# A state recurrence moved from per-head steps to whole tiles on two engines, and a filter cut into token chunks

## The chip, the cores and the metric

The kernel runs on one core of a Trainium2 chip. The metric is the device time of one execution, in microseconds (us). The kernel before takes 2790.79 us (median of 3 runs, 2787.46 to 2793.94). The engines are named as the profile names them: PE (TensorE, matrix products), DVE (VectorE), ACT (ScalarE), POOL (GpSimd) and SP (SyncE, which here issues the DMAs). Each works through its own queue in order.

## The reference, cut to what matters

Two layers of a mixer run over 128 context tokens and 1024 latent tokens of width 1024. Each layer normalises and modulates `x` to `h`, projects it, and computes three branches, which are gated, merged and added to `x`:

```
y_conv = ba * short_conv(ca * xa, conv_w) * silu(ga)     # 3 taps along the tokens
o_na   = neighbourhood attention (latent) or plain attention (context)
s_new  = exp(b_last) * s + sum over the chunk of k~ v    # gated linear attention: state per head
o      = q~ s + (masked q k) v                           # what a chunk reads of the state
merged = g_conv*(y_conv @ wb[0]) + g_na*(y_na @ wb[1]) + g_gla*(y_gla @ wb[2])
x      = x + gate * (merged @ w_out)
```

The linear attention has 4 heads, with a state of 64 x 128 each, and runs in both directions. The changed lines compute the state recurrence and the three taps.

## The kernel before, in words

All large products are made of float32 pairs (a rounded part `hi` and its remainder `lo`), three matmuls each. A weight block is loaded to `wraw` by SP, rounded to `whi` by ACT and its remainder `wlo` is made by POOL (`split_w`, L182 and L183); each of the three tiles has three buffers. `mode_a` multiplies one weight block of 128 columns with one chunk of 384 tokens: 24 matmuls into a `ps` bank, of which there are two. The third matmul of each such product is the first that reads `wlo`. A bank is free again when its result has been read ("evacuated").

The tokens are cut into 3 chunks of 384. The convolution runs over 4 blocks of 128 features. In a block PE first makes `xa` and `ca` for each chunk (ACT copies `xa`, DVE multiplies the two to `u`, L1289), then `ba` and `ga` for each chunk (DVE makes `y`, L1301, and, behind ACT's tanh, `th`, L1309; POOL multiplies the two, L1310). Between the halves DVE filters `u` to `cv` over all 1154 columns (L1292 to L1294).

Beside this main work runs a side work in the same PE queue: the linear attention (`gla`) and then the neighbourhood attention. A planner (`Pace`) counts the expected time of PE's main work and lets the side work take a step whenever its credit reaches one; `pace.wait(us)` lets the side work pause for so much of the planner's time. When `gla` ends, the planner sets the rate of the attention's steps so that they end some 20 us before the main work does. PE's order is that of the code. The order of the other engines is set by a scheduler.

`gla` goes over 9 chunks of 128 tokens and leaves in `su` what each chunk adds to the state (L1121). Then comes the recurrence: 8 steps, forward in partitions 0 to 63 and backward in 64 to 127. In a step the new state `gs` is the old one times `dec` plus `su` (L1161, for each head and direction one DVE instruction on 64 x 128), and the old state times `al` is written to `su` (L1163 on POOL for the backward half, L1166 on ACT for the forward half). The state's tiles have four buffers in turn. Behind the pause PE multiplies `su` with the queries and DVE adds the result to `o` (L1193). `o` is then normalised, behind a branch on a flag (`fi`) that every engine takes.

Of the kernel before, what the change touches and what calls it, by code (L numbers as in the profile page):

```python
# [7 lines left out]
F32 = mybir.dt.float32  # L8
# [3 lines left out]
ALU = mybir.AluOpType  # L12
# [9 lines left out]
T = TP + TL  # L22
NT = T // 128
NCH = 3
CH = 384
# [4 lines left out]
GH = 4  # L30
DK = 64
DV = 128
# [80 lines left out]
def hybrid_step(ctx: ExitStack, tc: tile.TileContext, io: dict):  # L113
    nc = tc.nc
    act, dve, gps, pe, sp = nc.scalar, nc.vector, nc.gpsimd, nc.tensor, nc.sync
    pace = Pace()
# [27 lines left out]
    C = {}  # L144
# [3 lines left out]
    def rsqrt(v, n, scale, tag):  # L148

        a = st.tile([128, n], F32, name="rs_a", tag=f"rsa{tag}")  # L150
        dve.tensor_scalar(a, v, scale, EPS, op0=ALU.mult, op1=ALU.add)  # L151
        y = st.tile([128, n], F32, name="rs_y", tag=f"rsy{tag}")
        gps.tensor_tensor(y, a, mhalf[:, 0:n], op=ALU.pow)  # L153
        u = st.tile([128, n], F32, name="rs_u", tag=f"rsu{tag}")
        dve.tensor_tensor(u, y, y, op=ALU.mult)
        dve.tensor_tensor(u, u, a, op=ALU.mult)
        dve.tensor_scalar(u, u, -0.5, 1.5, op0=ALU.mult, op1=ALU.add)
        r = st.tile([128, n], F32, name="rs_r", tag=f"rsr{tag}")
        dve.tensor_tensor(r, y, u, op=ALU.mult)
        return r  # L160
# [25 lines left out]
    def load_w(pieces, nk, lo_engine=gps):  # L186
        return split_w(*raw_w(pieces, nk), lo_engine)
# [35 lines left out]
    def mode_a(wts, src, nk, c):  # L223

        wh, wl = wts
        ps = mm.tile([128, 512], F32, name="ps", tag="mm")
        n = 0
        for k in range(nk):
            hh, hl = src[c][0][:, k, :], src[c][1][:, k, :]
            for a, b in ((wh, hh), (wh, hl), (wl, hh)):  # L230
                mul_(ps[:, 0:CH], a[:, k, :], b, 0.163, start=n == 0, stop=n == 3 * nk - 1)
                n += 1
        return ps[:, 0:CH]
# [294 lines left out]
    def layer(l):  # L528
# [21 lines left out]
        def side():  # L550
            yield from gla(l, d)
            left = main0 + main_us - pace.main
            pace.rate = NH * 23 / max(left - 20.0, 40.0)
            yield from attention(l, d)
# [15 lines left out]
        for m in range(4):  # L570
            conv(l, m, win, fw, cvp, d.yd[0])
# [458 lines left out]
    def gla(l, d):  # L1030
# [5 lines left out]
        dec = g0.tile([128, NT, GH], F32, name="dec")  # L1036
# [114 lines left out]
        S = g1.tile([128, GH, DV], F32, name="gs", tag="la")  # L1151
        sp.dma_start(S[0:64], io["state_fwd"][0, l].rearrange("h k v -> k h v"))
        sp.dma_start(S[64:128], io["state_bwd"][0, l].rearrange("h k v -> k h v"))
        for i in range(8):
            nS = g1.tile([128, GH, DV], F32, name="gs", tag=("qk1", "la")[i % 2])
            for s, c in ((0, i), (1, 7 - i)):
                r = slice(64 * s, 64 * s + 64)
                u = su[r, c, :].rearrange("p (h v) -> p h v", h=GH)
                if i < 7:
                    for h in range(GH):  # L1160
                        dve.scalar_tensor_tensor(nS[r, h], S[r, h], dec[r, c + 1, h:h + 1], u[:, h], op0=ALU.mult, op1=ALU.add)  # L1161
                if s:
                    gps.tensor_tensor(u, S[r], al[r, c + 1, :, 0:1].to_broadcast([64, GH, DV]), op=ALU.mult)  # L1163
                else:
                    for h in range(GH):
                        act.mul(u[:, h], S[r, h], al[r, c + 1, h, 0:1])  # L1166
            S = nS
# [13 lines left out]
        for c in range(NCH):  # L1181
            o3 = g2.tile([128, 3, BW], F32, name="o3", tag="o3", bufs=3)
            sp.dma_start(o3, d.oid[c * CH:(c + 1) * CH, :].rearrange("(t p) c -> p t c", p=128))
            O.append(o3)
        yield from pace.wait(20.0)
        for c in range(1, NT):
            load_q(c + 2)
            qt, o = qts[c], O[c // 3][:, c % 3, :]
# [11 lines left out]
        for c, o3 in enumerate(O):  # L1200
# [3 lines left out]
            r = rsqrt(red, 12, 1.0 / DV, "q")  # L1204
# [67 lines left out]
    def segs(c):  # L1272

        return ((0, 128, 0), (128, 256, 130)) if c == 0 else ((0, 384, CH * c + 2),)

    def conv(l, m, win, fw, cvp, yd):
        wx = load_w([win(XA + m * 128, 128)], KD)
        wc = load_w([win(CA + m * 128, 128)], KD)
        u = cvp.tile([128, T + 4], F32, name="u", tag="u", bufs=1)
        gps.memset(u[:, 0:1], 0.0)  # L1280
        gps.memset(u[:, 129:131], 0.0)
        gps.memset(u[:, T + 3:T + 4], 0.0)
        for c in range(NCH):
            ps = mode_a(wx, H, KD, c)
            xa = cvp.tile([128, CH], F32, name="xa", tag="xa")
            act.copy(xa, ps)
            ps = mode_a(wc, H, KD, c)
            for o, n, p in segs(c):
                dve.tensor_tensor(u[:, p + 1:p + 1 + n], ps[:, o:o + n], xa[:, o:o + n], op=ALU.mult)  # L1289
        cv = cvp.tile([128, T + 2], F32, name="cv", tag="cv", bufs=1)  # L1290
        w = lambda i: C["conv_w"][:, l, m, i:i + 1]
        dve.tensor_scalar(cv, u[:, 0:T + 2], w(0), None, op0=ALU.mult)  # L1292
        dve.scalar_tensor_tensor(cv, u[:, 1:T + 3], w(1), cv, op0=ALU.mult, op1=ALU.add)
        dve.scalar_tensor_tensor(cv, u[:, 2:T + 4], w(2), cv, op0=ALU.mult, op1=ALU.add)  # L1294
        wb = load_w([win(BA + m * 128, 128)], KD)
        wg = load_w([win(GA + m * 128, 128)], KD)
        for c in range(NCH):
            ps = mode_a(wb, H, KD, c)
            y1 = fw.tile([128, CH], F32, name="y1", tag="y1")
            for o, n, p in segs(c):  # L1300
                dve.tensor_tensor(y1[:, o:o + n], ps[:, o:o + n], cv[:, p:p + n], op=ALU.mult)  # L1301
            ps = mode_a(wg, H, KD, c)
            keep(yd)(c, m, silu2_times(ps, y1, fw, "th"))

    def silu2_times(ps, y1, fw, tag):

        th = fw.tile([128, CH], F32, name="th", tag=tag)
        act.activation(th, ps, ACTF.Tanh, scale=0.5)
        dve.scalar_tensor_tensor(th, th, 1.0, ps, op0=ALU.add, op1=ALU.mult)  # L1309
        gps.tensor_tensor(th, th, y1, op=ALU.mult)  # L1310
        return th

    def keep(yd):
        def f(c, m, y):
            sp.dma_start(yd[m * 128:(m + 1) * 128, c * CH:(c + 1) * CH], y)
        return f
# [225 lines left out]
```

## Time and profile before

| | |
|---|---|
| median of the timed runs | 2790.79 us |
| the profiled execution | 2797.96 us |
| its span, first to last instruction | 2796.2 us |
| PE busy | 2710.4 us (97%) |
| DVE busy | 1192.1 us (43%) |
| POOL busy | 1038.9 us (37%) |
| ACT busy | 954.0 us (34%) |
| granted TensorE clock, mean | 0.991 |

PE is the engine that sets the time: it is busy 97% of the span. The three other engines have time over on the mean, but each works in order, and PE waits wherever one of them delivers late. So the places where PE sits idle are to be looked for, and what stood in front of the late instruction on its engine. The first layer's convolution and recurrence stand around 350 to 600 us, its attention from about 600 to 1130 us; the second layer has the same 1385 us later.

### The profile page before, as it was taken

The numbers are of one execution on the slowest core, as the hardware profiler recorded it, in microseconds if no ns is written. First come the engines' busy times: TensorE is split into PE (matmuls) and PEld (weight loads), VectorE is DVE, ScalarE is ACT, GpSimd is POOL, SyncE is SP. The second block draws the span as 40 slices with busy tenths as digits, with TensorE's granted clock in tenths as the row PEclk, the third lists the DMA queues.
The fourth block names the chain that finished last, engine by engine and source line by source line (L and its number), as shares of the span: only waits on it lengthen the run. The fifth ranks groups of instructions, "written<-read, shape, count | busy, mean of one in ns | idle before, by whom it ended". The sixth has DMA issues, their size and how long they took to land. (4 is left out here: it accounts for less than half of the span.)

```text
span 2796.2 us, 47972 instructions
## 1 busy us (share of the span) xinstructions
PE 2710.4 (97%) x18548; PEld 2654.7 (95%) x18548; DVE 1192.1 (43%) x2391; ACT 954.0 (34%) x1820; POOL 1038.9 (37%) x884
## 2 busy tenths in 40 slices
PE   6999999999999999999989999999999999999999
PEld 4999999999999999999989999989999999999999
DVE  5345335545444443335173453364553334433341
ACT  6244322223444433312152442222344343342121
POOL 0343233453574431167343332333642112212852
PEclk8999999999999999999999999999999999999999
DMA  7444672364665653555243447623655555435551
GB/s 234 119 137 121 202 230 71 114 178 139 169 180 154 171 155 92 180 177 168 89 127 111 126 121 227 212 67 126 173 151 148 142 139 155 135 109 177 168 180 69
DMA packets 455740, 415.26 MB, mean 149 GB/s; under 512 B 84740, under 2 KB 422028, under 8 KB 455248
## 3 DMA queue, kind: packets, MB, share of 16 engines
q1 hardware_dynamic: 455504, 412.13, 49.9%
q8 instruction: 146, 2.39, 0.4%
q14 instruction: 90, 0.74, 0.1%
HBM read 292.04 MB, written 136.74 MB: 153 GB/s over the span
## 5 line engine op out<-in xcount | busy, mean ns | idle before, releaser
L131 PE MATMUL ps<-hhi,whi 128*128 128x384 f32 x2496 | 851.5, 341 | 20.5 <-DVE y L1301 6.5
L131 PE MATMUL ps<-hhi,wlo 128*128 128x384 f32 x2496 | 848.1, 340 | 0.3 <-PEq L1196 0.3
L131 PE MATMUL ps<-hlo,whi 128*128 128x384 f32 x2496 | 848.1, 340 | 0.0
L183 POOL TENSOR_TENSOR wlo<-wraw,whi 128x1024 fp32r<-128x1024 f32 (+2 forms) x172 | 369.3, 2147 | 828.8 <-ACT whi L182 751.2
L131 PE MATMUL ps<-wlo,hhi 128*128 128x256 f32 (+1 forms) x1984 | 567.9, 286 | 7.0 <-DVE wlo L183 7.0
L131 PE MATMUL ps<-whi,hhi 128*128 128x256 f32 (+1 forms) x1984 | 567.9, 286 | 4.4 <-DVE ro L617 2.4
L131 PE MATMUL ps<-whi,hlo 128*128 128x256 f32 (+1 forms) x1984 | 567.5, 286 | 0.0
L131 PEld LDWEIGHTS ps<-hhi,whi 128*128 128x128 f32 x2496 | 471.2, 189 | 29.7 <-DVE th L1309 6.7
L131 PEld LDWEIGHTS ps<-hlo,whi 128*128 128x128 f32 x2496 | 471.1, 189 | 2.1 <-issue 1.4
L131 PEld LDWEIGHTS ps<-hhi,wlo 128*128 128x128 f32 x2496 | 471.2, 189 | 1.8 <-issue 0.9
L131 PEld LDWEIGHTS ps<-wlo,hhi 128*128 128x128 f32 x1984 | 380.9, 192 | 9.0 <-DVE wlo L183 8.1
L131 PEld LDWEIGHTS ps<-whi,hhi 128*128 128x128 f32 x1984 | 381.0, 192 | 7.4 <-PE ps L131 3.1
L131 PEld LDWEIGHTS ps<-whi,hlo 128*128 128x128 f32 x1984 | 380.9, 192 | 0.6 <-issue 0.3
L182 ACT CAST whi<-wraw 128x1024 fp32r<-128x1024 f32 (+1 forms) x200 | 189.5, 949 | 323.8 <-PE ps L131 251.2
L964 DVE TENSOR_TENSOR ptl<-psb,pth 128x640 fp32r<-128x640 f32 x128 | 105.3, 823 | 189.4 <-ACT pth L963 189.3
L935 ACT ACTIVATE prob<-prob,mn 128x640 f32<-128x640 f32 x128 | 106.3, 830 | 190.4 <-DVE mn L934 190.1
L934 DVE CUSTOM_DVE_ANT_0 prob<-psb,bt 128x640 f32<-128x640 f32 x128 | 105.2, 822 | 97.6 <-PE psb L131 84.2
L296 POOL TENSOR_SCALAR adapr<-wraw,scond 128x256 f32<-128x256 f32 x112 | 110.3, 984 | 94.2 <-DMA wraw<-in_w_ada 44.7
L131 PE MATMUL ps<-yh,whi 128*128 128x384 f32 x384 | 131.2, 342 | 4.4 <-DVE mx L1389 3.0
L153 POOL TENSOR_TENSOR rs_y<-rs_a,mhalf 128x12 f32<-128x12 f32 (+2 forms) x42 | 78.3, 1864 | 141.0 <-DVE rs_a L151 134.9
L131 PE MATMUL ps<-yl,whi 128*128 128x384 f32 x384 | 130.0, 339 | 0.0
L131 PE MATMUL ps<-yh,wlo 128*128 128x384 f32 x384 | 130.0, 339 | 0.0
(220 smaller groups left out, 3605.2 us busy)
## 6 DMA issues: line engine op xcount, KB each, us to landing
wraw<-in_w_in SPq DMA_DIRECT2D x88, 512.0 KB, 4.4
gd<-gt SPq DMA_DIRECT2D x144, 192.0 KB, 2.2
gl<-gd SPq DMA_DIRECT2D x144, 192.0 KB, 2.7
wraw<-in_w_gate SPq DMA_DIRECT2D x48, 512.0 KB, 4.7
wraw<-in_w_ada SPq DMA_DIRECT2D x32, 512.0 KB, 4.0
qt<-qld SPq DMA_DIRECT2D x128, 128.0 KB, 3.1
vt<-vw SPq DMA_DIRECT2D x64, 256.0 KB, 3.3
wraw<-in_w_branch SPq DMA_DIRECT2D x48, 256.0 KB, 3.0
```

Of the source, the lines that this page charges most:

```text
L131: pe.matmul(out, lhsT, rhs, **kw)
L153: gps.tensor_tensor(y, a, mhalf[:, 0:n], op=ALU.pow)
L182: act.copy(hi[:, 0:n], raw[:, 0:n])
L183: lo_engine.tensor_tensor(lo[:, 0:n], raw[:, 0:n], hi[:, 0:n].bitcast(F32), op=ALU.subtract)
L296: gps.tensor_scalar(pr, rv[:, kk], w, None, op0=ALU.mult)
L934: dve.tensor_tensor_reduce(p[:, 0:n], ps[:, lo:lo + n], bias, 1.0, 3e38, ALU.add, ALU.min, mn)
L935: act.activation(p[:, 0:n], p[:, 0:n], ACTF.Exp, bias=mn, scale=-1.0, accum_out=sums)
L964: dve.tensor_tensor(to[1], src, to[0].bitcast(F32), op=ALU.subtract)
```

## The change

Three parts, in both layers alike. First, a step of the recurrence handles all four heads with two instructions on 64 x 512, a multiply with `dec` and an add of `su`: the forward half on DVE, the backward half on POOL. Second, the pause behind the recurrence is 45 instead of 20 us of the planner's time. Third, the filter of a convolution block is made for each chunk of tokens by itself, as soon as the next chunk's `u` is there, into three tiles `cv` instead of one.

```diff
                 if i < 7:
-                    for h in range(GH):
-                        dve.scalar_tensor_tensor(nS[r, h], S[r, h], dec[r, c + 1, h:h + 1], u[:, h], op0=ALU.mult, op1=ALU.add)
+                    eng = gps if s else dve
+                    eng.tensor_tensor(nS[r], S[r], dec[r, c + 1, :].unsqueeze(2).to_broadcast([64, GH, DV]), op=ALU.mult)
+                    eng.tensor_tensor(nS[r], nS[r], u, op=ALU.add)
...
-        yield from pace.wait(20.0)
+        yield from pace.wait(45.0)
...
+        taps = {}
+
+        def filtered(c):
+
+            a = CH * c + 2 if c else 0
+            n = CH * (c + 1) + 2 - a
+            cv = cvp.tile([128, CH + 2], F32, name="cv", tag="cv", bufs=3)
+            w = lambda i: C["conv_w"][:, l, m, i:i + 1]
+            dve.tensor_scalar(cv[:, 0:n], u[:, a:a + n], w(0), None, op0=ALU.mult)
+            for i in (1, 2):
+                dve.scalar_tensor_tensor(cv[:, 0:n], u[:, a + i:a + i + n], w(i), cv[:, 0:n], op0=ALU.mult, op1=ALU.add)
+            taps[c] = cv, a
+
...
-        cv = cvp.tile([128, T + 2], F32, name="cv", tag="cv", bufs=1)
-        w = lambda i: C["conv_w"][:, l, m, i:i + 1]
-        dve.tensor_scalar(cv, u[:, 0:T + 2], w(0), None, op0=ALU.mult)
-        dve.scalar_tensor_tensor(cv, u[:, 1:T + 3], w(1), cv, op0=ALU.mult, op1=ALU.add)
-        dve.scalar_tensor_tensor(cv, u[:, 2:T + 4], w(2), cv, op0=ALU.mult, op1=ALU.add)
+            if c:
+                filtered(c - 1)
+        filtered(NCH - 1)
...
-                dve.tensor_tensor(y1[:, o:o + n], ps[:, o:o + n], cv[:, p:p + n], op=ALU.mult)
+                cv, a = taps[c]
+                dve.tensor_tensor(y1[:, o:o + n], ps[:, o:o + n], cv[:, p - a:p - a + n], op=ALU.mult)
```

Line numbers of after are up to 13 higher behind the change: `y` is L1314 there, `th` L1322 on DVE and L1323 on POOL, `u` L1303, the product of the backward state L1164. The names in the rows below are those of the tiles; a number behind one is that of its buffer.

DVE in the second convolution block of the first layer, from the last `su` (L1121) on, before:

```order
L1121 TENSOR_TENSOR su<-psm,al 128x512
L1161 SCALAR_TENSOR_TENSOR gs<-gs,dec,su 64x128 x16
L1301 TENSOR_TENSOR y_5305<-ps,cv 128x384
L1161 SCALAR_TENSOR_TENSOR gs<-gs,dec,su 64x128 x17
L1309 SCALAR_TENSOR_TENSOR th<-th,ps 128x384
L1161 SCALAR_TENSOR_TENSOR gs<-gs,dec,su 64x128 x10
L1301 TENSOR_TENSOR y_5490<-ps,cv 128x384
```

And the same place of the changed kernel:

```order
L1121 TENSOR_TENSOR su<-psm,al 128x512
L1161 TENSOR_TENSOR gs<-gs,dec 64x512
L1314 TENSOR_TENSOR y_5321<-ps,cv 128x384
L1162 TENSOR_TENSOR gs<-gs,su 64x512
L1161 TENSOR_TENSOR gs<-gs,dec 64x512
L1162 TENSOR_TENSOR gs<-gs,su 64x512
L1322 SCALAR_TENSOR_TENSOR th<-th,ps 128x384
L1161 TENSOR_TENSOR gs<-gs,dec 64x512
L1314 TENSOR_TENSOR y_5478<-ps,cv 128x384
L1162 TENSOR_TENSOR gs<-gs,su 64x512
```

In front of each evacuation (`y`, `th`) there stood 10 to 17 small steps; now there stand one to three larger instructions.

POOL at the same place, before: behind the `th` of the block's first chunk the products of the backward state, and between them the remainders `wlo` of the next block's two first weights (`wraw` and `whi` are the raw and the rounded weights):

```order
L1310 TENSOR_TENSOR th<-th,y_5219 128x384
L1163 TENSOR_TENSOR su<-gs,al 64x512 x5
L1310 TENSOR_TENSOR th<-th,y_5305 128x384
L1163 TENSOR_TENSOR su<-gs,al 64x512
L183 TENSOR_TENSOR wlo<-wraw,whi 128x1024
L1163 TENSOR_TENSOR su<-gs,al 64x512 x2
L183 TENSOR_TENSOR wlo<-wraw,whi 128x1024
L1310 TENSOR_TENSOR th<-th,y_5490 128x384
```

And in the changed kernel, behind the same first `th`:

```order
L1162 TENSOR_TENSOR gs<-gs,su 64x512
L1164 TENSOR_TENSOR su<-gs,al 64x512
L1161 TENSOR_TENSOR gs<-gs,dec 64x512
L1162 TENSOR_TENSOR gs<-gs,su 64x512
L1164 TENSOR_TENSOR su<-gs,al 64x512
L1161 TENSOR_TENSOR gs<-gs,dec 64x512
L1162 TENSOR_TENSOR gs<-gs,su 64x512
L1323 TENSOR_TENSOR th<-th,y_5321 128x384
L1164 TENSOR_TENSOR su<-gs,al 64x512
L1161 TENSOR_TENSOR gs<-gs,dec 64x512
L1162 TENSOR_TENSOR gs<-gs,su 64x512
L183 TENSOR_TENSOR wlo<-wraw,whi 128x1024
```

Six products and one `th` stood in front of the first `wlo`; now six products, four adds and one `th` do. Two more products stand between it and the second `wlo`, before and now.

PE where it first multiplies `su` with the queries (`gq2`), before in the third block's first half (row 2971 of PE's queue):

```order
L131 MATMUL ps_5592<-hlo_200,whi_5524 128x384
L131 MATMUL ps_5592<-hhi_199,wlo_5525 128x384
L131 MATMUL psm_5607<-su_3625,gq2_5434 128x128 x4
L131 MATMUL ps_5592<-hhi_199,whi_5524 128x384
L131 MATMUL ps_5592<-hlo_200,whi_5524 128x384
```

And in the changed kernel, in the third block's second half (row 3130):

```order
L131 MATMUL ps_5795<-hlo_200,whi_5706 128x384
L131 MATMUL ps_5795<-hhi_199,wlo_5707 128x384
L131 MATMUL psm_5801<-su_3625,gq2_5422 128x128 x4
L131 MATMUL ps_5795<-hhi_199,whi_5706 128x384
L131 MATMUL ps_5795<-hlo_200,whi_5706 128x384
```

The product moved back by 159 rows, and all that follows it in the side work with it; the matmuls around it are the same main work.

## Rows read from the trace of the kernel before

**Rows 1.** Busy time by stretch: recurrence and attention, first and second layer.

```profile
core 0: us, PE busy (x) PEld busy (x) DVE busy (x) ACT busy (x) POOL busy (x), PEclk, DMA share, GB/s
455.00:600.00 145.00, 137.62 (x838) 135.26 (x838) 80.56 (x124) 36.26 (x64) 68.50 (x57) 0.99 0.39 116
600.00:1130.00 530.00, 519.27 (x3255) 511.68 (x3254) 240.69 (x524) 212.33 (x415) 226.00 (x206) 0.99 0.55 153
1840.00:1985.00 145.00, 139.52 (x851) 137.16 (x850) 80.55 (x124) 37.48 (x66) 69.66 (x57) 0.99 0.38 115
1985.00:2515.00 530.00, 527.23 (x3305) 521.11 (x3304) 215.85 (x455) 213.72 (x416) 130.11 (x95) 1.00 0.52 144
```

**Rows 2.** Waits of PE, 455 to 600 us: total us, times, longest.

```profile
PE ps L131 <- DVE y L1301: 4.2, 3, 2.9
PE ps L131 <- DVE th L1309: 3.0, 1, 3.0
```

**Rows 3.** Timeline of DVE behind the last `su`: start us, us, instructions [idle before].

```profile
473.86 0.69 DVE L1121 TENSOR_TENSOR su<-psm,al 128x512 f32<-128x512 f32 x1 [1.35 <-PE psm L131]
474.58 6.95 DVE L1161 SCALAR_TENSOR_TENSOR gs<-gs,dec,su 64x128 f32<-64x128 f32 x16
481.46 0.54 DVE L1301 TENSOR_TENSOR y<-ps,cv 128x384 f32<-128x384 f32 x1
482.03 6.86 DVE L1161 SCALAR_TENSOR_TENSOR gs<-gs,dec,su 64x128 f32<-64x128 f32 x17
488.92 0.56 DVE L1309 SCALAR_TENSOR_TENSOR th<-th,ps 128x384 f32<-128x384 f32 x1
489.51 6.71 DVE L1161 SCALAR_TENSOR_TENSOR gs<-gs,dec,su 64x128 f32<-64x128 f32 x10
496.25 0.56 DVE L1301 TENSOR_TENSOR y<-ps,cv 128x384 f32<-128x384 f32 x1
```

**Rows 4.** Timeline of PE, first layer.

```profile
480.50 0.33 PE L131 MATMUL ps<-hlo,whi 128*128 128x384 f32 x1
480.67 0.33 PE L131 MATMUL ps<-hhi,wlo 128*128 128x384 f32 x1
...
482.06 0.44 PE L131 MATMUL ps<-hhi,whi 128*128 128x384 f32 x1 [0.53 <-DVE y L1301]
...
508.97 1.05 PE L131 MATMUL psm<-su,gq 128*128 128x128 f32 x8
```

**Rows 5.** Busy time and granted clock by stretch, behind the stops.

```profile
497.00:503.00 6.00, 6.00 (x26) 6.00 (x27) 0.75 (x2) 0.74 (x3) 5.38 (x4) 0.72 1.04 350
503.00:506.00 3.00, 3.00 (x19) 3.00 (x18) 0.00 (x0) 0.41 (x1) 0.00 (x0) 1.00 1.04 399
1868.00:1884.00 16.00, 11.16 (x52) 10.53 (x53) 15.24 (x31) 8.23 (x22) 6.99 (x6) 0.89 0.11 33
```

**Rows 6.** By line and shape, POOL and DVE: count | busy us, mean ns | idle.

```profile
L183 POOL TENSOR_TENSOR wlo<-wraw,whi 128x1024 fp32r<-128x1024 f32 x122 | 297.5, 2439 | 667.9 <-ACT whi L182 605.2 <-DMA bt<-t2d 19.5 <-PE ps L131 14.9
L1310 POOL TENSOR_TENSOR th<-th,y 128x384 f32<-128x384 f32 x48 | 49.3, 1027 | 80.8 <-DVE th L1309 74.0 <-issue 4.1 <-DVE rs_u L155 2.7
L1098 POOL TENSOR_TENSOR am<-am 128x512 f32<-128x512 f32 x18 | 23.0, 1280 | 101.9 <-DVE am L1097 91.8 <-PE ps L131 5.5 <-DMA qk<-qkd 4.5
L1163 POOL TENSOR_TENSOR su<-gs,al 64x512 f32<-64x512 f32 x16 | 16.9, 1061 | 21.7 <-DVE gs L1161 18.9 <-issue 2.8
L1193 DVE TENSOR_TENSOR o<-o,psm 128x512 f32<-128x512 f32 x16 | 11.0, 687 | 28.9 <-PE psm L131 26.6 <-DMA gq<-qtd 2.3
```

**Rows 7.** Timelines of DVE and POOL around a filter, first layer.

```profile
461.95 3.43 DVE L1293 SCALAR_TENSOR_TENSOR cv<-u,conv_w,cv 128x1154 f32<-128x1154 f32 x1
465.42 1.42 DVE L1294 SCALAR_TENSOR_TENSOR cv<-u,conv_w,cv 128x1154 f32<-128x1154 f32 x1
461.26 2.90 POOL L183 TENSOR_TENSOR wlo<-wraw,whi 128x1024 fp32r<-128x1024 f32 x1
```

**Rows 8.** Waits of PE in the first attention stretch, the longest.

```profile
PE psb L135 <- DVE ptl L964: 4.8, 2, 4.3
```

## The prediction

> **What bounds the kernel now.** I read the busy time by stretch first. TensorE (PE) is busy nearly always, so a change can only win what PE loses: from 455 to 600 us it is busy 137.62 of 145 us and in the same stretch of the second layer, 1840 to 1985, 139.52: 7.4 and 5.5 us idle. The two attention stretches behind them lose 10.7 and 2.8 us [rows 1]. Then the waits of PE inside the first layer's stretch, to see who ends that idle time: VectorE (DVE), with an evacuation of the convolution, `y` (L1301, 4.2 us) or `th` (L1309, 3.0 us); that is 7.2 of the 7.4 [rows 2]. The second layer runs the same code, and I take its 5.5 us for the same. PE waits nowhere for the state itself.
>
> Then DVE's timeline there, to see why an evacuation of 0.55 us comes late [rows 3]. The last `su` ends at 473.86 + 0.69 = 474.55. Behind it stand 16 small state steps (6.95 us), one `y`, 17 steps (6.86), one `th`, 10 steps (6.71), one `y`. DVE works in order, `ps` has two banks, and one product is 24 matmuls 0.17 us apart, 4.2 us [rows 4]: each evacuation may stand 4.2 us behind its product, and here about 7 us of steps stand between two of them. So PE stops at 481.53 (482.06 less its wait of 0.53), then twice more.
>
> A second loss follows: in the 6 us after the stops the granted clock is 0.72 of full (part of the time at 1.2 instead of 2.4 GHz), in the second layer 0.89 over 16 us; a stretch at full clock, like the 3 us behind the first, reads 1.00 [rows 5]. 6 x 0.28 and 16 x 0.11 give about 1.7 us each. What the change can win in the two stretches is thus 7.4 + 5.5 + 2 x 1.7 = 16 us, less the 0.2 us a layer that these waits don't explain: 15.9 us.
>
> **The state recurrence.** Behind the last `su`, DVE loses 44 steps (20.9 us, of which the three groups here are 20.5 [rows 3]) and gets 8 instructions on 64x512: four multiplies, four adds. The trace of before has neither. The nearest row is `o` (L1193, 128x512) with 0.69 us; the other end is four of the old steps at 0.43 each, 1.74 [rows 3, 6]. I take 0.69, the same element count per partition: 5.5 us where 20.9 stood. The order shows at most three of them in front of an evacuation, 2.1 us. So the old stops go, if these instructions need not wait for GpSimd (POOL).
>
> POOL gets the other half, 14 instructions a layer. The broadcast product there costs 1.06 (L1163), a sum of two full tiles 1.28 (L1098) [rows 6]. POOL's chain can't begin before 474.55, since its first add reads the last `su`. Queued behind it is what matters: `wlo` of the next block's first weights, the twelfth row of the piece of order. In front of it are four adds, six products and one `th`: 4 x 1.28 + 6 x 1.06 + 1.03 = 12.5 us; `wlo` takes 2.44 [rows 6]. It is ready at 474.55 + 14.9 = 489.5. PE without stops needs it with the third matmul of that product: 481.53 + 48 x 0.174 + 0.35 = 490.2. So with undisturbed engines it just fits: late is nothing.
>
> But they disturb each other. A filter step of DVE that takes 1.42 us alone took 3.43 beside a `wlo` on POOL, and that `wlo` took 2.90 [rows 7]. DVE's six state instructions in front of this `wlo` therefore add up to 6 x 0.69 = 4.1 us to POOL's chain: ready at 493.6, PE 3.4 us late. The second `wlo` has two more products in front of it, 2.1 + 2.4 = 4.6 us against PE's 4.2: another 0.4. Bounds of the new stop: 0 to 3.8 us a layer. I take 1.7, since POOL also idles for `th`, when DVE can pass: 3.4 us in both layers. A fall of the clock behind so short a stop is left out here; rival 1 has it.
>
> The Trainium skill says of this (SBUF — State Buffer, Who interferes with whom) that a VectorE instruction with two SBUF inputs and a GpSimd instruction that reads SBUF exclude each other, and that the later one waits for the whole of the other. The old `y` and `th` have one input in PSUM and are untouched by this rule; all new DVE instructions have two in SBUF, so it speaks against this change. The 3.43 against 1.42 agrees; by the rule in full the new stop would be at the upper bound above, without it at the lower.
>
> **The pause.** From 20 to 45 on the planner's clock. PE's first product with `su` moves back by 159 rows (the piece of order): 159 x 0.174 = 27.7 us, from 508.97 to about 530 once 7 us of stops are gone. POOL's whole chain from 474.55: 7 adds, 14 products, 2 `th`, 2 `wlo` = 9.0 + 14.8 + 2.1 + 4.9 = 30.8, with eight DVE instructions 36.3: done by 511. PE does not wait for it, 19 us to spare; with the old pause and no stops it would have come at 502 and waited 9. Behind the pause the normalisation of `o` moves from the third convolution block into the fourth, beside the sums for the next modulation. In the order each `u` still stands in front of where PE needs it; cost nothing, hidden by two `ps` banks; a late `u` there would cost 1 to 2 us a layer, which I keep for the range.
>
> Attention ends with the main work as before, but starts 27 us later: the same 72 items in some 500 instead of 530 us, 5% denser. PE's work there is the same. Its idle time, 10.7 and 2.8 us [rows 1], is a matter of which `ptl`, cast or bias load collides (4.8 us of the first are two waits for `ptl` [rows 8]); the collisions are drawn anew. From both sides: -6 (the 4.3 us wait and its clock fall vanish) to +13.5 (all idle time doubles). I take +2.
>
> **The filter by chunks.** Nine instructions for three, the same columns: six fixed parts more. 128x384 against 128x512 (0.55 and 0.69 [rows 3, 6]) leave 0.14 us for an instruction without columns: 0.8 us of DVE a block, beside PE, with DVE busy 80.6 of 145 us [rows 1]. Behind the last `u` only four of the nine are left. What is left of the first layer's `y` waits beside the stops, 4.2 - 0.5 - 2.9 = 0.8 us, lies at this place of the fourth block [rows 2]; it is in the 15.9. SP's and POOL's queues get nothing from this part.
>
> **The sum.** -15.9 + 3.4 + 2 = -10.5 us. Against the profiled execution, 2797.96 (span 2796.2 and 1.8 around it), that is 2787.5; its own time lies 7 us above the median of the timed runs, so I apply the difference to that median: 2790.79 - 10 = 2781.
>
> **Rivals.**
> 1. POOL becomes the bound in the recurrence: `wlo` 3.8 us late in each layer, and the clock falls after it as it did after 3.0 us: 2 x (3.8 + 1.7) = 11 of 15.9 us come back, with the +2 of attention: -3, 2788. For it: the 3.43 us [rows 7], and POOL's in-order queue; against: PE's slack holds if POOL gets the port at once. 0.22.
> 2. Slower: the denser attention. One mechanism: the chain from scores to `ptl` (DVE, ACT, DVE, PE, ACT, DVE) is late for its slot, since the slots are 5% closer while the weights, casts and modulation sums beside it are not. The other terms give -12.5, so it eats the gain once the idle time of the two attention stretches doubles (13.5 us more) and is a loss that can be measured from 18 us more on; at +20 the time is 2798. Against: PE idles 2.8 of 530 us in the second layer, so there is slack. 0.12.
> 3. The attention falls well: its 4.3 us wait goes too, and no `wlo` is late: -15.9 - 5: 2770. 0.14.
> 4. The change doesn't do what it says: `su` is late in spite of the pause and PE waits; needs POOL 19 us behind my sum, then no gain: 2791. 0.02.
>
> **How the numbers follow.** Forecast 0.50, 2774 to 2786 by the bounds of its terms. A measurement here tells 0.2%, 5.6 us, from no change: faster is below 2785.2, slower above 2796.4. Faster: 0.48 of the forecast, 0.14 of rival 3, some 0.06 of rival 1: 0.68. Slower: 0.11. Same: the rest, 0.21. The range goes from rival 3 to just short of rival 2: 2771 to 2795.
>
> **What would show it.** Right: no PE wait for `y` or `th` between 474 and 500 us nor at its place in the second layer; the granted clock 1.00 there; DVE busy some 15 us less around 474 to 497; a new PE wait of 0 to 4 us for POOL's `wlo` at the start of the third block; none for `su`. Wrong: a `wlo` wait over 4 us, any wait of PE for DVE's `o`, or idle time in the attention stretches above 25 us together. If the stops go and the time doesn't fall by 5 us, the attention stretches must show where it went.

## The result, and the profile after

The changed kernel takes 2837.37 us (median of 6 runs, 2827.34 to 2841.42), the one before 2790.42 beside it (6 runs, 2787.46 to 2793.94): a ratio of 1.0155, 95% interval 1.0138 to 1.0171. By the ratio it is 43 us slower (47 by the medians), where 10 us faster were forecast.

The profiled execution has a span of 2839.3 us against 2796.2. PE is busy 2721.8 instead of 2710.4 us, at a mean granted clock of 0.984 instead of 0.991; so 31.7 of the 43.1 us are idle time of PE and 11.4 are longer matmuls. The busy time by stretch says where, in the columns of [rows 1]:

```profile
455.00:600.00 145.00, 136.65 (x811) 134.32 (x810) 77.52 (x106) 32.43 (x57) 84.32 (x63) 0.96 0.29 89
600.00:1130.00 530.00, 505.06 (x3144) 497.27 (x3143) 236.56 (x508) 205.86 (x404) 227.68 (x212) 0.98 0.57 157
1840.00:1985.00 145.00, 140.04 (x858) 137.29 (x857) 65.61 (x93) 33.65 (x66) 68.60 (x55) 0.96 0.25 80
1985.00:2515.00 530.00, 510.84 (x3185) 503.08 (x3184) 222.05 (x459) 205.42 (x398) 149.80 (x113) 0.99 0.52 144
```

The second layer stands some 21 us later in the changed kernel, so that a stop of its fourth block (at 2000 us) falls out of the third stretch into the fourth. Moved by 21 us the two read:

```profile
1861.00:2006.00 145.00, 136.54 (x809) 134.00 (x808) 77.57 (x106) 32.33 (x57) 84.23 (x63) 0.96 0.29 89
2006.00:2536.00 530.00, 514.34 (x3217) 507.25 (x3216) 211.28 (x446) 209.32 (x406) 132.33 (x101) 0.99 0.52 142
```

In the recurrence PE thus idles 8.4 and 8.5 us, where [rows 1] gave 7.4 and 5.5: nothing was won. In the attention stretches it idles 24.9 and 15.7 us, where it idled 10.7 and 2.8. The waits of PE over the whole run (total us, times, longest) name them:

```profile
PE ps L131 <- DVE th L1347: 23.8, 2, 12.0
PE psb L135 <- DVE ptl L964: 9.7, 4, 4.3
PE ps L131 <- DVE u L1303: 9.7, 4, 3.2
...
PE ps L131 <- ACT xa L1300: 6.4, 3, 2.9
...
PE ps L131 <- DVE y L1314: 0.4, 1, 0.4
PE ps L131 <- POOL wlo L183: 0.4, 1, 0.4
```

The old waits for `y` and for `th` in the convolution [rows 2] are gone, and the feared wait for `wlo` is 0.4 us. In their place stand four kinds of stop, each once a layer.

**The start of attention: 12 us for `th` (L1347).** This `th` belongs to the stage behind the convolution, which stores one every 4.2 us. The timeline of SP there, first layer (start, us, instructions):

```profile
623.29 0.39 SPq L173 DMA_DIRECT2D wraw<-in_w_in  x1
...
625.89 10.11 SPq L862 DMA_DIRECT2D bt<-t2d  x16
...
636.69 0.59 SPq L877 DMA_DIRECT2D vraw<-in_cache_v  x1
...
639.74 0.45 SPq L1328 DMA_DIRECT2D y0d<-th  x1
```

And that of ACT, with what ended each idle time:

```profile
632.20 1.04 ACT L182 CAST whi<-wraw 128x1024 fp32r<-128x1024 f32 x1 [7.60 <-DMA bt<-t2d]
638.83 0.30 ACT L879 CAST vc<-vraw 128x128 fp32r<-128x128 f32 x1 [5.58 <-DMA vraw<-in_cache_v]
643.00 0.96 ACT L1346 ACTIVATE th<-ps 128x384 f32<-128x384 f32 x2 [3.87 <-DMA y0d<-th]
```

Sixteen loads of the bias tile `bt` occupy SP for 10 us; behind them stand the load of `vraw`, on which ACT waits with a cast in its queue, and the store `y0d<-th`, on which the next `th` waits for its buffer, since there are two. PE stops from 632.3 to 644.1. In the kernel before the same loads stood elsewhere:

```profile
586.05 8.81 SPq L862 DMA_DIRECT2D bt<-t2d  x16
...
596.95 0.43 SPq L1315 DMA_DIRECT2D y0d<-th  x1
```

There they stand between the last `u` of the fourth convolution block (DVE at 585.47) and the store of its first `th`, where PE waits under 1 us. The pause moved them.

**The fourth block: 3.2 us for `u`.** The normalisation of `o`, moved there by the pause, stands in front of `u` on DVE:

```profile
588.83 2.35 DVE L157 TENSOR_SCALAR rs_u<-rs_u 128x12 f32<-128x12 f32 x1
591.22 0.65 DVE L159 TENSOR_TENSOR rs_r<-rs_y,rs_u 128x12 f32<-128x12 f32 x1
591.90 1.76 DVE L1207 TENSOR_TENSOR o<-o,rs_r 128x1536 f32<-128x1536 f32 x1
593.57 0.55 DVE L1303 TENSOR_TENSOR u<-ps,xa 128x384 f32<-128x384 f32 x1
```

Its first instruction has 12 columns and takes 2.35 us, as long as the `wlo` that runs on POOL beside it from 588.54 (2.61 us).

**In front of the recurrence: 1.6 to 1.8 us for `u`.** POOL now has a state multiply in front of the all-reduce of the flag `fa`:

```profile
450.35 1.50 POOL L1161 TENSOR_TENSOR gs<-gs,dec 64x512 f32<-64x512 f32 x1
457.45 0.38 POOL L1147 PARTITION_ALL_REDUCE fa<-fm  x1 [5.59 <-PE psm L135]
457.86 0.15 DVE L1149 TENSOR_SCALAR fi<-fa 128x1 int32<-128x1 f32 x1 [6.91 <-POOL fa L1147]
```

DVE idles 6.91 us for `fa`, and `u` stands behind. The all-reduce starts 5.6 us after POOL's last instruction, as it did before the change (5.7 us there); the multiply moves it back, and the order on DVE now has the flag ahead of `gqt`, `gkt` and `u`. The Trainium skill (GPSIMD Engine Reference, Instruction dispatch) says that a freshly loaded GpSimd routine first pays about 6 us with no instruction in the profile; the 5.6 us agree, behind two instructions that configure POOL (`MODIFY_POOL_CONFIG`, at 451.8).

**In the recurrence: 2.9 us for `xa`.** DVE's and ACT's timelines, then the clock behind the stop:

```profile
487.87 1.51 DVE L1161 TENSOR_TENSOR gs<-gs,dec 64x512 f32<-64x512 f32 x1 [0.94 <-POOL su L1164]
489.42 1.67 DVE L1162 TENSOR_TENSOR gs<-gs,su 64x512 f32<-64x512 f32 x1
...
493.85 1.52 DVE L1161 TENSOR_TENSOR gs<-gs,dec 64x512 f32<-64x512 f32 x1 [2.30 <-POOL su L1164]
...
502.03 2.76 DVE L1162 TENSOR_TENSOR gs<-gs,su 64x512 f32<-64x512 f32 x1
```

```profile
504.83 2.44 ACT L1167 ACTIVATE su<-gs,al 64x128 f32<-64x128 f32 x8 [5.12 <-DVE gs L1162]
507.18 0.46 ACT L1300 COPY xa<-ps 128x384 f32<-128x384 f32 x1
```

```profile
508.00:514.00 6.00, 6.00 (x20) 6.00 (x20) 2.81 (x3) 0.00 (x0) 5.77 (x6) 0.52 0.95 320
644.00:650.00 6.00, 5.87 (x18) 5.87 (x19) 0.55 (x2) 0.00 (x0) 0.00 (x0) 0.50 1.10 307
```

Where [rows 3] had groups of steps without a gap, DVE now waits between them. A state instruction takes 1.3 to 1.7 us beside POOL and the last one 2.76 beside a `wlo` (501.53, 2.72), against 0.68 alone (at 448.04); [rows 7] had shown the same of a filter. And DVE waits for POOL: a state tile's buffer is free only when POOL's product (L1164) has read the old state. So ACT's products come late, the last ones behind the 2.76 us, and `xa` behind them. In the 6 us after this stop and after the one for `th` the clock is 0.52 and 0.50 of full (0.72 in [rows 5]), the lower of the two levels (1.2 GHz) for nearly all of the time; at the same places of the second layer it is 0.50 and 0.74.

### The profile page after: what moved, and what is told of

Read it like the earlier page. It is cut to its first block, busy times and chain, and to the rows that moved or that the text cites. A ratio compares the mean times of both kernels' runs of the same rounds, so it can differ in the third digit from the quotient of the medians.

```text
span 2839.3 us, 47971 instructions
## 1 busy us (share of the span) xinstructions
PE 2721.8 (96%) x18548; PEld 2665.4 (94%) x18548; DVE 1193.7 (42%) x2355; ACT 953.4 (34%) x1820; POOL 1086.1 (38%) x912
## 5 line engine op out<-in xcount | busy, mean ns | idle before, releaser
L131 PE MATMUL ps<-hhi,whi 128*128 128x384 f32 x2496 | 858.3, 344 | 46.1 <-DVE th L1347 23.8
L296 POOL TENSOR_SCALAR adapr<-wraw,scond 128x256 f32<-128x256 f32 x112 | 120.1, 1072 | 95.5 <-DMA gate_d<-gate_s 36.4
```

What stands on the lines that cost most here:

```text
L131: pe.matmul(out, lhsT, rhs, **kw)
L296: gps.tensor_scalar(pr, rv[:, kk], w, None, op0=ALU.mult)
```

## The experiments

Each batch has its own runs of the kernel before (medians 2795.9 to 2800.2 us); ratios are to those, with 95% intervals.

**e1, the pause alone.**

```diff
-        yield from pace.wait(20.0)
+        yield from pace.wait(45.0)
```

> The kernel before with the pause of 45 instead of 20 alone. Theory (the pause): it moves the start of attention, with its burst of bias loads in SP's queue, onto the second half of the fourth convolution block, where PE needs a th every 4.2 us, and the normalisation of o into that block's first half. Both stops of the changed kernel must be here: a wait of PE for th of about 12 us and one for u of about 3 us in each layer, with the clock falls behind them some 2 x 17 = 34 us: 2815 to 2830 us. Rival 1 (GpSimd's half of the recurrence is what costs): no new stop, 2786 to 2795. Rival 2 (the denser attention costs, wherever it starts): 2800 to 2815, in many waits under 5 us within attention.

2845.27 us, 1.0163 (1.0143 to 1.0182): 45 us slower, above the theory's band. The `th` wait at the start of attention is the theory's, and the recurrence is the old one. The `u` wait of 3 us did not come; in the fourth block PE waits for `ott` (2.8 and 2.2 us) and for `y` instead:

```profile
PE ps L131 <- DVE th L1334: 20.4, 2, 10.9
...
PE psb L135 <- DVE ptl L964: 9.1, 3, 4.1
PE ps L131 <- DVE y L1301: 8.2, 6, 2.4
PE psm L131 <- ACT pth L963: 7.2, 4, 3.2
...
PE psm L135 <- ACT ott L1214: 5.3, 3, 2.8
```

So the pause by itself costs as much as the whole change. GpSimd's half isn't needed for it, against rival 1.

**e2, the recurrence alone; e3, the filter alone; e4, the changed kernel with the pause of 20.**

```diff
-                    for h in range(GH):
-                        dve.scalar_tensor_tensor(nS[r, h], S[r, h], dec[r, c + 1, h:h + 1], u[:, h], op0=ALU.mult, op1=ALU.add)
+                    eng = gps if s else dve
+                    eng.tensor_tensor(nS[r], S[r], dec[r, c + 1, :].unsqueeze(2).to_broadcast([64, GH, DV]), op=ALU.mult)
+                    eng.tensor_tensor(nS[r], nS[r], u, op=ALU.add)
```

> The kernel before with the new recurrence alone (pause 20, filter in one piece). Theory (the pause): the old stops for y and th go (-15.9 us), the new ones for u and xa come (2 x 1.7, 2 x 2.9 and three clock falls of 1.7: +14), and no th wait at the start of attention: 2786 to 2794; if PE now comes to its first product with su before GpSimd's chain is through, a wait for su of up to 9 us a layer on top, up to 2808. Rival 1 (GpSimd's half): 2815 to 2835. Rival 2 (denser attention): 2780 to 2794, since the rate of attention is that of the kernel before.

> The kernel before with the filter by token chunks alone. The prediction priced it at nothing: 2787 to 2794, with the y wait of 0.8 us in the fourth block gone and the stops of the recurrence where they were. No theory of the loss asks for more than 2 us here.

> The changed kernel with its pause set back from 45 to 20. Theory (the pause): the th wait of 12 us and the u wait of 3 us in the fourth block go in both layers, 2 x 17 = 34 us: 2795 to 2808, the same as the new recurrence alone but for 3 us. Rival 1 (GpSimd's half): within 8 us of the changed kernel, 2829 to 2841. Rival 2 (denser attention): 15 to 25 us under the changed kernel, with the th wait still there.

e2: 2810.14 us, 1.0036 (1.0021 to 1.0051), 10 us slower. e3: 2800.60, 1.0003 (0.9989 to 1.0017), nothing. e4: 2810.04, 1.0049 (1.0028 to 1.0069), 14 us slower by the ratio (10 by the medians), with no `th` wait at the start of attention. Both fall where the theory of the pause put them, e2 with the wait for `su`. The waits of PE in e2:

```profile
PE psm L131 <- POOL su L1164: 10.5, 2, 6.1
...
PE ps L131 <- ACT xa L1287: 5.8, 2, 2.9
...
PE ps L131 <- DVE u L1290: 3.8, 2, 2.1
```

They are the `xa` wait and the first `u` wait of the changed kernel, and a wait for `su` that the longer pause covers. So the new recurrence is no gain at either pause: what it takes from DVE it loses through POOL, to 20.1 us of these waits, where `y` and `th` together cost 12.6 in the kernel before (6.5 and 6.1).

**e6, both halves of the new recurrence on DVE.**

Against e2:

```diff
-                    eng = gps if s else dve
+                    eng = dve
```

> The kernel before with the state on 64x512 instructions for both halves on DVE, nothing on GpSimd; pause 20, filter in one piece. Theory (GpSimd's half costs through DVE, ACT and the last product): the waits of PE for u behind the all-reduce, for xa and for su, which the new recurrence alone showed, all go; each DVE instruction is back at 0.68 us; 28 of them (19 us) stand where the old steps took 23, four to six in front of an evacuation, so that y and th waits of 0 to 2 us remain: 5 to 12 us faster than before. Rival (it is the form of the instructions or the tightened chain that costs, not GpSimd): the xa and u waits stay, 5 to 12 us slower than before, like the new recurrence alone.

2796.20 us, 1.0000 (0.9985 to 1.0014). The waits for `u`, `xa` and `su` are gone, as the theory said of POOL's half. But `th` costs 8.8 us (four waits, up to 3.7), more than expected, and the gain of 5 to 12 us did not come. The `th` that stops PE stands on ACT, behind products that wait for state instructions of DVE; two of these took 3.50 us beside a `wlo` there (491.43; the `wlo` 490.93, 2.73).

**e5 and e9, the changed kernel with another start of attention.** e5 puts the bias loads behind the first items' loads and hands them out; e9 takes ACT's two waits away as well.

```diff
-        load_bias(0, 0, 3)
         for i in range(2):
             ahead(i)
-        yield from pace.wait(16.0)
+        until = pace.clock + 16.0
+        for g in range(2):
+            for r in range(8):
+                load_rows(0, 0, 3, g, r)        # one of the sixteen loads
+                if r % 3 == 2 and not pace.draining:
+                    yield
+        while pace.clock < until and not pace.draining:
+            yield
...
-            act.copy(vc[:, :, 0, :], raw)                                    # e9
+            gps.tensor_copy(vc[:, :, 0, :], raw)
...
-            th = fw.tile([128, CH], F32, name="th", tag="th")                # e9
+            th = (fw, cvp)[(3 * m + c) % 2].tile([128, CH], F32, name="th", tag=("th", "xa")[(3 * m + c) % 2])
```

> The changed kernel, its pause of 45 kept, with the sixteen bias loads at the start of attention behind the loads of the first two items and handed out three at a time, a step of the planner between, within the 16 us that the kernel waits there anyway. Theory (the burst): the two th waits of 12 us go down to under 3 us each and their clock falls with them: 20 to 30 us faster than the changed kernel, so 13 to 25 us slower than the one before. Rival (attention put later is slow in itself, by its rate or by what it meets there, whatever the order of the loads): the waits stay, or come back elsewhere in attention, and the time stays within 8 us of the changed kernel.

> e5 (the changed kernel with the bias loads handed out), and two things more that the trace of e5 shows in front of the late th: the silus stage's th takes four buffers in turn instead of two (the two more are those of xa, unused by then), so that ACT need not wait for a store to land, and vc is cast on GpSimd instead of ACT, so that ACT does not stand before a load. Theory (the stop is a matter of queues at the start of attention): the th wait of 5.5 us in each layer goes to under 1, some 11 us of waits and 4 of clock less than e5: 0 to 17 us slower than the kernel before. Rival (a later attention costs whatever is done to its start): within 4 us of e5, 26 to 34 us slower than before.

e5: 2829.16 us, 1.0107 (1.0069 to 1.0144); the `th` wait falls from 23.8 to 10.7. e9: 2830.97, 1.0113 (1.0096 to 1.0131); it falls to 2.0, and the time does not. So e5 gains 13 us on the changed kernel (1.0155), between its theory and its rival, and e9 is its rival's. The wait has moved on:

```profile
PE psb L135 <- DVE ptl L968: 20.8, 5, 6.9
...
PE ps L131 <- DVE u L1313: 10.2, 4, 3.3
...
PE ps L131 <- DVE th L1357: 2.0, 2, 1.4
```

Some 35 us later SP and ACT in e9 read:

```profile
657.10 5.45 SPq L860 DMA_DIRECT2D bt<-t2d  x11
...
667.29 0.38 SPq L173 DMA_DIRECT2D wraw<-in_w_gate  x1
```

```profile
671.62 1.04 ACT L182 CAST whi<-wraw 128x1024 fp32r<-128x1024 f32 x1 [11.27 <-DMA wraw<-in_w_gate]
672.57 0.82 ACT L939 ACTIVATE prob<-prob,mn 128x640 f32<-128x640 f32 x1
```

A weight load stands on SP behind the next head's bias loads (issued at 667.29, 4.3 us before its cast starts), its cast stands on ACT in front of the exponential, and PE waits 5.8 us for `ptl`. My theory that the stop at the start was the cost fell here: removed, most of it is given back at the next load.

**e12, the same start with the pause alone.** The pause of e1 and the start of e9, on the old recurrence.

> The kernel before with the pause of 45 and the start of attention of e9 (bias loads handed out three at a time, th with four buffers, vc on GpSimd); old recurrence, filter in one piece. Theory (SP's queue, full of each head's bias loads, is what a later attention meets): the th wait is under 1 us, PE waits 5 to 7 us for ptl in each layer some 40 us later behind the next head's loads, as in e9, and the time stays 25 to 36 us over before. Rival (the th stop was the cost, and e9 kept only what the new recurrence costs): 5 to 15 us over before.

2818.66 us, 1.0083 (1.0059 to 1.0107): 23 us over before, between the two expectations. There the start does take half of the 45 us away. `ptl` costs 15.8 us (4.8 before [rows 8]), `ott` 5.2 and `y` 8.0 (6.5).

**e13 and e14, the bias tiles of the first head only.** Pause 20 and 45, with the start of e9 and without the reloads:

```diff
-                if g == 1 and j in (0, 3) and h + 1 < NH:
-                    load_bias(h + 1, *((0, 1) if j == 0 else (1, 3)))
```

> The kernel before (pause 20) with the start of attention of e9, and the bias tiles loaded for the first head only: the reloads for the seven other heads of each layer are left out, 224 loads a layer. It is the partner of e14. Theory (SP's queue): the kernel before loses little to these loads where attention starts early, so 0 to 10 us faster than before. Rival (attention itself): the same as before within 4 us.

> e13 with the pause of 45. Theory (SP's queue): without the reloads the later attention costs little, within 12 us of e13, and the ptl wait 40 us into attention is gone. Rival (attention itself, its density or its place in the queues of DVE and ACT): 25 to 36 us over e13, as e12 is over before.

Both kernels leave out loads that the result needs; they only measure. e13: 2785.59 us, 0.9963 (0.9950 to 0.9976). e14: 2807.44, 1.0038 (1.0024 to 1.0052). The reloads cost about 10 us with either pause, and the later attention still costs 22 us without them (2807.4 less 2785.6), as it cost 23 with them. So the reloads are not its cause, against my theory. In e14 a stop some 25 us into attention reads so on SP and ACT:

```profile
644.00 0.43 SPq L173 DMA_DIRECT2D wraw<-in_w_gate  x1
```

```profile
652.52 1.04 ACT L182 CAST whi<-wraw 128x1024 fp32r<-128x1024 f32 x1 [8.65 <-DMA wraw<-in_w_gate]
...
653.88 0.69 ACT L965 CAST pth<-psb 128x640 fp32r<-128x640 f32 x1
```

The load is issued right behind those of the next head's keys and values and lands 8.5 us later, and ACT holds attention's casts behind it; PE waits 4.7 us for `ptl`, and 7.2 in the second layer. With 5.5 for `ott` in the fourth block that is 17.4 of the 20.3 us by which PE idles longer in the profiled execution of e14 than in that of e13 (94.2 and 73.9); another 11.7 us there are longer matmuls. In e13 the same load is issued at 631.80, lands 3.8 us later and is not waited for: its cast starts at 645.03. The stretches around the two loads, first e13, then e14:

```profile
628.00:636.00 8.00, 8.00 (x52) 7.93 (x51) 4.22 (x8) 4.25 (x7) 2.40 (x1) 1.00 0.54 165
640.00:650.00 10.00, 10.00 (x63) 9.97 (x62) 2.12 (x6) 1.30 (x3) 0.00 (x0) 1.00 1.10 254
```

The DMA share is 0.54 in the one and 1.10 in the other, where ACT already stands at the cast (from 643.87) when SP issues the load. So in e14 the load is issued too late and meets full DMA engines. Whether an earlier load of that weight would end it was not tried.

**e7 and e8, one state step behind each evacuation.** e6, with a step's `dec` made by a small instruction that reads the last evacuated tile, and steps 4 us apart; e8 has the start of e5 as well.

```diff
+            gate[0] = st.tile([128, GH], F32, name="gz")          # behind each y, th, u
+            dve.tensor_scalar(gate[0], x[:, 0:GH], 0.0, None, op0=ALU.mult)
...
+                        dve.tensor_tensor(dg[r], dt, gate[0][r], op=ALU.add)
+                yield from pace.wait(4.0)
```

> As e6, and each step of the state takes its dec through a small instruction that reads four columns (times zero) of the last evacuated tile, so that one step stands behind each evacuation, y, th or u, not several in front of one; the steps are handed out 4 us of the planner's time apart and the pause behind them is 4.5, which puts PE's first product with su and all of attention some 14 us later than before. Theory (DVE's order bounds the recurrence, and a late attention meets the stores): no y, th, u or xa wait over 1 us between 455 and 530 us; but the burst of bias loads falls into the second half of the fourth block, a th wait of 2 to 6 us in each layer there: between 10 us faster than before and the same. Rival (the old stops come back wherever DVE is over 90% busy): waits of 5 us a layer in the third block's first half, 0 to 8 us slower.

> As e7, with the bias loads handed out as in e5. Theory: neither the old stops nor the th wait of the burst: 10 to 16 us faster than before, all that PE lost in the recurrence. Rival (attention put 14 us later costs in itself): as e7, within 3 us.

e7: 2822.91 us, 1.0084 (1.0051 to 1.0117), and 23.6 us of `th` waits are back at the start of attention. e8: 2816.26, 1.0071 (1.0047 to 1.0096), with 10.4 of them. Both theories missed. PE's first product with `su` comes at 534.7 in e7 (509.0 before), 147 rows back and not 14 us: nearly the 159 rows of the changed kernel. And the gates did not end the stops of the recurrence: in each layer of e7 PE waits 2.0 us for `th` and 2.3 behind a gate (`gz`), where the kernel before lost 4.4 to 5.9 in its two longest. Again a later attention costs.

**e10, e11 and e15, gates without a later attention.** e10 gates the last three steps only and takes their waits out of the pause; e11 adds the start of e9; e15 makes the last four forward products on GpSimd.

```diff
+            if i in {3: 4.0, 4: 4.0, 5: 4.0}:
+                yield from pace.wait(4.0)
...
-                if s:                                                # e15
+                if s or i >= 4:
                     gps.tensor_tensor(u, S[r], al[r, c + 1, :, 0:1].to_broadcast([64, GH, DV]), op=ALU.mult)
```

> e6 (both halves of the state on DVE, pause 20), with the last three steps gated as in e7, each behind another evacuation, and the waits between them taken out of the pause, so that PE's first product with su comes at nearly the same row as before (12 rows, 2 us, later). Theory (order on DVE, and on ACT behind it, is what stops PE in the recurrence; attention starts where it did): the th wait of 3.7 us a layer of e6 goes, no y, th, u, xa or su wait over 1 us from 455 to 530 us: 6 to 14 us faster than before. Rival (the step from last su to first product is bound by the chain itself): an su wait of 3 to 8 us a layer, the same as before or slower by up to 6.

> e10 with the start of attention of e9 (bias loads handed out, th with four buffers, vc on GpSimd). Theory: at this place of attention's start the burst cost nothing before, so within 4 us of e10. Rival (the loads handed out are later for the first scores, or GpSimd's cast delays its wlo): 3 to 10 us slower than e10.

> e10 with the forward products of the last four steps on GpSimd instead of ACT. In e10 ACT's th stood behind four products and a cast that waited for a state instruction of DVE, which a wlo on GpSimd had held for 3.5 us. Theory: the th wait of 4.0 us a layer goes (under 1.5), with the clock fall behind it, 6 to 12 us faster than before. Rival (GpSimd is the bound then): a wlo wait of 2 to 5 us a layer at the start of the third block, or an su wait, within 3 us of before.

e10: 2799.52 us, 1.0003 (0.9993 to 1.0013). e11: 2799.52, 1.0011 (1.0000 to 1.0021). e15: 2798.48, 1.0011 (0.9996 to 1.0026). None gains. In e10 a `th` wait of 4.0 us a layer stays: ACT's `th` stands behind products and a cast, and these behind two multiplies of DVE that take 3.50 us (491.97). e15 takes that away and leaves 2.6 us, now on DVE:

```profile
493.30 3.50 DVE L1167 TENSOR_TENSOR gs<-gs,dg 64x512 f32<-64x512 f32 x2
496.83 1.40 DVE L1168 TENSOR_TENSOR gs<-gs,su 64x512 f32<-64x512 f32 x2
498.26 0.56 DVE L1325 SCALAR_TENSOR_TENSOR th<-th,ps 128x384 f32<-128x384 f32 x1
```

Two multiplies take 3.50 us beside a `wlo` (493.32, 2.92), and in the second layer PE waits 2.5 us for `su` from POOL.

**e16 and e17, the bias reloads on other queues.** The kernel before with the start of e5, the reloads issued by GpSimd or by ACT.

In effect:

```diff
-            sp.dma_start(bass.AP(tensor=dst.tensor, ...
+            gps.dma_start(bass.AP(tensor=dst.tensor, ...              # e17: act
```

> The kernel before (pause 20) with the first head's bias loads handed out three at a time and the reloads for the other heads issued by GpSimd instead of SP. Theory (SP's queue is what the reloads cost): most of the 10 us of e13 come, 4 to 10 us faster than before. Rival (the bytes, or GpSimd held by the loads' waits in front of its wlo): the same within 4 us, or slower by 5 to 20 us with PE waits for wlo.

> As e16, with the reloads issued by ACT, behind the exponential that reads the same scores, so that their wait for the bias tile is over when they come up. Theory (SP's queue): 2 to 10 us faster than before. Rival (ACT in order is held up by issuing sixteen loads): 10 to 40 us slower, with PE waits for pth, ptl and th.

e16: 2866.72 us, 1.0239 (1.0212 to 1.0267): 448 of these loads occupy POOL for 225.7 us. e17: 2822.16, 1.0085 (1.0063 to 1.0108), with 13.4 us of waits for `gt` from ACT and 16.9 for `th`. e17 is its rival's; e16 is 68 us slower, far beyond its own, with 17.6 us of waits for `whi` and 8.7 for `wlo`. Of the three queues SP is the best place for them. But for e13, which leaves out work, no kernel here beats the one before.

## Why the prediction was wrong

**The old stops: right, and worth nothing.** They went as priced. What failed in this term is its condition, "if these instructions need not wait for GpSimd (POOL)". They do: by the buffers of the state tile (0.2 to 2.6 us at a time), and each takes 1.3 to 2.8 us where I took 0.69. I put the mutual exclusion on POOL's chain alone, to see whether `wlo` is late. It came in time (0.4 us, where 3.4 were priced); the delay went to DVE, from there to ACT's products, and `xa` stood behind these. The prediction weighs ACT's queue nowhere. e6 shows it from the other side: without POOL's half these waits go. On the rule that the prediction quoted (the Trainium skill, SBUF — State Buffer, Who interferes with whom): the doubled state instructions agree with it; the 2.35 us of a 12-column instruction beside a `wlo` do not follow from it, since that one reads a single tile in SBUF. Nor does the rule speak against the change alone: the old steps read two tiles there too, and in [rows 3] the last ten, with a `wlo` beside them (492.52, 2.37), took 0.67 us each, the others 0.40 to 0.43.

**The all-reduce: not seen.** One POOL instruction moved ahead of it and DVE's queue stood for 6.9 us; PE lost 3.4 us by it in both layers together.

**The pause at no cost: the step that decided.** In the sum the pause has no term of its own beside the +2 for attention. "Cost nothing, hidden by two `ps` banks" was said of the normalisation of `o` in the fourth block, and that cost 6.3 us of `u` waits in the two layers, with 1 to 2 us a layer kept for the range. Worse, the pause was priced by what PE, POOL and DVE do behind it, and not by the DMAs that move with it. The start of attention issues 16 bias loads and the loads of its first items in one piece on SP; the prediction has nothing on SP's queue at that place. e1 settles that the pause alone costs 45 us; e4, with 20, that it costs some 30 within the new recurrence, where it also covers the `su` wait (9.1 us in e4).

**"I take +2" for attention: the size, and the bound.** The collisions were drawn anew, as said, but the upper bound of 13.5 assumed that idle time doubles; it tripled, from 13.5 to 40.6 us in the two stretches, 27.1 more where 2 were taken. (Over 25 us was the prediction's own sign of being wrong.) Term by term, forecast and measured: idle time of PE in the recurrence -9.1 us (12.5 of old stops less 3.4 of new ones) and +4.0; attention +2 and +27.1; longer matmuls -3.4 and +11.4, since the sum has no term for the clock behind new stops. Rival 2 had the sign and put the loss in the spacing of the slots. Shown is: about half of what the pause alone costs (e1 against e12, 22 us) lies in the order, the buffers and the cast at the start of attention, which e12 changed together; within the new recurrence the same start gave back 12 us (e9). The other half, 22 to 23 us, stays with the reloads and without them (e12; e13 against e14), and in e14 most of the added idle time is a late `ott` and a cast in front of attention's on ACT that waits for a weight load. That a denser attention as such costs anything was not shown.

**The filter: right.** Nothing (e3).

**What stays open.** Which of the two costs the wait for that weight load, its late issue or the full DMA engines, and so what an early start of attention avoids; and whether a late attention at a lower rate would cost less.

## What to carry to other kernels

Before you move a piece of side work, list the transfers that it issues in one go and lay them over the queue of the engine that issues them at the new place: a store that frees a buffer and a load that a cast waits for count as much as the matmuls. When you split a chain over two engines, follow the buffers that tie the halves and every queue behind them, the third engine's too. And when a stop is taken away, look whether the time falls: in e9 9 us of waits went and came back at the next load.

## What the runs showed of the hardware

- Two state instructions of DVE, 0.69 us each alone, took 3.50 us beside a `wlo` of 2.92 on GpSimd (e15); one of 12 columns took 2.35 (after), where 0.16 is its time alone.
- GpSimd's all-reduce starts 5.6 to 6.1 us after the instruction in front of it (both layers of before, after, e2 and e6), and the next one that GpSimd computes with comes 6.9 to 7.3 us behind it.
- After stops of 2.9 and 11.8 us the granted clock was 0.52 and 0.50 over 6 us (0.50 and 0.74 in the second layer), so the longer stop did not cost more clock; behind the stops of [rows 5] it was 0.72.
- A bias load issued by GpSimd occupied it for 0.51 us (448 loads, 225.7 us).
- The same weight load of 512 KB landed 3.8 us after its issue at a DMA share of 0.54 (e13) and 8.5 us after it at 1.10 (e14).
